# 1/rms of tokens: eleven VectorE steps and a diagonal, or one GpSimd power and a repeated column

## The chip, the cores and the metric

The kernel runs on one core of a Trainium2 chip. The metric is the device time in microseconds of one execution. The core has five engines with a queue each, worked off in order: PE (TensorE; PEld is its weight loading), DVE (VectorE), ACT (ScalarE), POOL (GpSimd) and SP, which here only issues DMAs.

## The reference

One layer of a hybrid decoder on 16 meta tokens and 1024 real tokens of width 1024, in float32. Three mixers run side by side on the normalised input, then a SwiGLU layer and a last normalisation follow:

```python
def rmsnorm(x, g):
    y = x * lax.rsqrt(jnp.mean(x * x, axis=-1, keepdims=True) + EPS)
    return y * g
...
hn = rmsnorm(h, mix_norm_g)
sb_q, sb_k, sb_v, ssm_z, ssm_xbc, ssm_dt, c_q, c_kv, k_r = split(hn @ w_in)
o_sb  = stick_breaking_attention(sb_q, sb_k, sb_v)      # 8 heads of 64
o_ssm = ssd_mixer(ssm_z, ssm_xbc, ssm_dt, ...)          # Mamba-2; ends in rmsnorm(y * silu(z), norm_g)
q  = rmsnorm(c_q,  q_norm_g)  @ w_uq                    # latents of width 384
kv = rmsnorm(c_kv, kv_norm_g) @ w_ukv                   # and of width 256
o_mla = mla_attention(q, kv, rope(k_r))                 # 8 heads
h = h + concat(o_sb, o_ssm, o_mla) @ w_out
fn = rmsnorm(h, ffn_norm_g)
h = h + (silu(fn @ w_gate) * (fn @ w_up)) @ w_down
return rmsnorm(h, final_norm_g)
```

So 1/rms per token is needed for the input, for both latents, for the gated state-space output, for the feed-forward input and for the output.

## The kernel before

Activations lie with features on the partitions and tokens along the free dimension. Each dense product is three TensorE products: operands are split into a rounded part and a rest (`hi`, `lo`), and hi·hi, lo·hi and hi·lo are added up in PSUM. ScalarE makes the rounded part; the rest is a subtraction, in most places on GpSimd.

The sum of squares of a token runs over partitions, so `token_rstd` takes it with TensorE: for each block of 128 tokens the squares are the weights and a column of ones moves, which leaves the sums as one column per block with tokens on the partitions (`ps`, up to 9 columns). `rstd_columns` then makes mean square plus epsilon on VectorE (L172), and `col_rsqrt` makes 1/√x there: a shift and a multiply-add on the bits for a first guess, and three Newton rounds of three instructions, all on a tile of 2 to 9 columns. `spread` turns the columns into a row repeated on all partitions: per block VectorE scales the identity by the column (`dg`, L180), and TensorE multiplies it with a tile of ones (L181).

Eleven places use this:

- `chunk_rstd`, three times, for the three token chunks of the input (pool `p0`, 3 blocks each). The first projections run on the input without 1/rms, and their results are scaled by `row` when they are taken out of PSUM (L585) or by the column `r` (L572); then `normalise` scales the input itself.
- `column_rstd`, three times: for both latents (`latent_units`), while the chunks of the state-space scan (`ssd_chunk`) run, and for the gate of its output (`gate_units`) beside the last attention heads. `spread_row` spreads them.
- `row_sums` and `row_spread`, twice, ahead of the feed-forward products, for each half of the tokens.
- `last_part` and `last_row`, three times, at the end, for 512, 256 and 256 tokens. The last of these takes its sums in PSUM banks of its own and calls `col_rsqrt` itself (tile `rl`).

A planner orders each engine's queue: it goes through the program with its own estimates of durations and takes what is ready and has priority. `tc.high_priority(offset=...)` moves instructions forward, and stands around most of the steps above. `tc.issue_after(ins)` puts the instructions of a block that are on the same engine behind `ins`. Around the feed-forward normalisations the order is steered by such marks:

```python
with tc.high_priority(offset=400):
    r = row_sums(acc)
    summed = last_on(PE)
    row = row_spread(*r)
    rowed, rowed_dve = last_on(PE), last_on(DVE)
```

`rowed_dve` is the last VectorE instruction there: before the change the last `dg`. The four VectorE instructions of L1406 stand behind it.

Of the kernel before, what the change touches and what calls it, by code (L numbers as in the profile page):

```python
# [11 lines left out]
F32 = mybir.dt.float32  # L12
F32R = mybir.dt.float32r
BF16 = mybir.dt.bfloat16
I32 = mybir.dt.int32
AF = mybir.ActivationFunctionType
ALU = mybir.AluOpType
AX = mybir.AxisListType
# [3 lines left out]
D = 1024  # L22
# [14 lines left out]
EPS = 1e-6  # L37
# [22 lines left out]
def tile_hybrid_block(ctx: ExitStack, tc: tile.TileContext, a: dict):  # L60
    nc = tc.nc
    act, dve, pool, pe, sp = nc.scalar, nc.vector, nc.gpsimd, nc.tensor, nc.sync
# [11 lines left out]
    const = ctx.enter_context(tc.tile_pool(name="const", bufs=1))  # L74
# [22 lines left out]
    ident = const.tile([128, 128], F32, name="ident")  # L97
# [3 lines left out]
    ones = const.tile([128, 128], F32, name="ones")  # L101
# [2 lines left out]
    dve.memset(zcol, 0.0)  # L104
    halfcol = const.tile([128, 1], F32, name="halfcol")
    dve.memset(halfcol, 0.5)
    sb_mask = const.tile([128, 128], BF16, name="sb_mask")
    mla_mask = const.tile([128, 128], BF16, name="mla_mask")
    for m, base in ((sb_mask, -1), (mla_mask, 0)):
# [30 lines left out]
            with tc.high_priority(offset=1000):  # L140
                evac(ps, c0, n)

    def col_rsqrt(r, x, tmp):

        ri, xi = r.bitcast(I32), x.bitcast(I32)
        dve.tensor_scalar(ri, xi, 1, None, ALU.arith_shift_right)
        dve.tensor_scalar(ri, ri, -1, 0x5F3759DF, ALU.mult, ALU.add)
        for _ in range(3):
            dve.tensor_tensor(tmp, r, r, op=ALU.mult)
            dve.scalar_tensor_tensor(tmp, x, -0.5, tmp, ALU.mult, ALU.mult)  # L150
            dve.scalar_tensor_tensor(r, tmp, 1.5, r, ALU.add, ALU.mult)

    def token_rstd(cols, ps, squares, blocks, width, bufs=1):


        for e, (t0, w) in enumerate(blocks):
            for i, sq in enumerate(squares):
                pe.matmul(
                    ps[:w, e : e + 1], sq[:, t0 : t0 + w], ones[:, 0:1], start=(i == 0), stop=(i == len(squares) - 1)
                )  # L160
        return rstd_columns(cols, ps, blocks, width, bufs)

    def rstd_columns(cols, ps, blocks, width, bufs=1):
        nb = len(blocks)
        x, r, t = (cols.tile([128, nb], F32, tag=f"rc{i}{nb}", bufs=bufs, name="rc") for i in range(3))
        e0 = 0
        if blocks[0][1] < 128:
            w = blocks[0][1]
            dve.memset(x[:, 0:1], 1.0)
            dve.tensor_scalar(x[:w, 0:1], ps[:w, 0:1], 1.0 / width, EPS, ALU.mult, ALU.add)  # L170
            e0 = 1
        dve.tensor_scalar(x[:, e0:nb], ps[:, e0:nb], 1.0 / width, EPS, ALU.mult, ALU.add)  # L172
        col_rsqrt(r, x, t)
        return r

    def spread(diag, row, r, blocks, t0, wide=None, bufs=2):

        for e, (b0, w) in enumerate(blocks):
            dg = diag.tile([128, 128], F32, tag="dg", bufs=bufs, name="dg") if wide is None else wide[:, 128 * e : 128 * (e + 1)]
            dve.tensor_scalar(dg[:w, :w], ident[:w, :w], r[:w, e : e + 1], None, ALU.mult)  # L180
            pe.matmul(row[:, b0 - t0 : b0 - t0 + w], ones[:w, :], dg[:w, :w], start=True, stop=True)  # L181

    dpool = ctx.enter_context(tc.tile_pool(name="dpsum", bufs=2, space=PSUM))
    tp_st = ExitStack()
# [2 lines left out]
    def bank():  # L187
        return dpool.tile([128, 512], F32, tag="d", name="d_ps")
# [10 lines left out]
    def fill_tile(tag, name):  # L199
        return fl.tile([128, 388 if tag == "craw" else 384], F32, tag=tag, name=name)  # L200
# [7 lines left out]
    p0 = p0_st.enter_context(tc.tile_pool(name="p0", bufs=1))  # L208
# [36 lines left out]
    def chunk_rstd(i):  # L245
        c0, n = CH_ALL[i]
        blocks = [(t0 - c0, w) for t0, w in BLOCKS[3 * i : 3 * i + 3]]
        acc = fill_tile("cacc", "acc")[:, :n]
        for k in range(KT):
            x = xT[:, k, c0 : c0 + n]  # L250
            sq = acc if k == 0 else sqs[k % 2][:, 512 * (k // 2 % 2) :][:, :n]
            act.activation(sq, x, AF.Square)
            if k > 0:
                dve.tensor_tensor(acc, acc, sq, op=ALU.add)
        ssum = ps0.tile([128, 4], F32, tag="ssum", name="ssum")
        with tc.high_priority(offset=200):
            r = token_rstd(p0, ssum, [acc], blocks, D, bufs=3)
            rrow = ps0.tile([128, 512], F32, tag="rrow", bufs=1, name="rrow")
            spread(p0, rrow, r, blocks, 0, bufs=3)
            row = fill_tile("craw", "row")  # L260
            act.copy(row[:, :n], rrow[:, :n])
        return r, row
# [373 lines left out]
    for i, (q0, qn) in enumerate(((0, 256), (256, 384), (640, 384))):  # L636
# [3 lines left out]
        c0, n = CH_ALL[i]  # L640
        r, row = stats[i]
# [59 lines left out]
    def spread_row(row, r, blocks, chunks, scale=1.0):  # L701
        for c0, m in chunks:
            ps = bank()
            inside = [e for e, b in enumerate(blocks) if c0 <= b[0] < c0 + m]
            spread(ga, ps, r[:, inside[0] : inside[-1] + 1], [blocks[e] for e in inside], c0)
            act.activation(row[:, c0 : c0 + m], ps[:, :m], AF.Copy, scale=scale)

    def heads(ap, h=8):
# [2 lines left out]
    ga = ctx.enter_context(tc.tile_pool(name="ga", bufs=1, side="right", reuse_waits="tile"))  # L711
    grow = ga.tile([128, T], F32, name="grow")
    with ExitStack() as st:
# [118 lines left out]
        def row_tile(name):  # L832
            return la.tile([128, T], F32, tag="lraw", bufs=4, name=name)
# [39 lines left out]
        for b, (t0, w) in enumerate(BLOCKS):  # L873
            ps = bank()
# [6 lines left out]
            t = row_tile("vtok")  # L881
# [18 lines left out]
        for c0, n in CH_SHORT:  # L900
# [4 lines left out]
            for half, (op, ta, tb) in enumerate(((ALU.subtract, ct, sn), (ALU.add, sn, ct))):  # L905
                t = fill_tile("cacc", "rope")
# [155 lines left out]
    def ffn_bank():  # L1062
        return pp.tile([128, 512], F32, tag="b", name="b_ps")
# [8 lines left out]
    def add(out, x, y, eng=None):  # L1072
        (eng or dve).tensor_tensor(out, x, y, op=ALU.add)  # L1073
# [10 lines left out]
    def q_tile(name):  # L1084
        return tq.tile([128, 512], F32, tag="q", name=name)

    def row_sums(squares):
        blocks = [(128 * b, 128) for b in range(4)]
        r = token_rstd(ga, bank(), squares, blocks, D)
        return r, blocks  # L1090

    def row_spread(r, blocks):
        ps = bank()
        spread(None, ps, r, blocks, 0, q_tile("dg"))
        return ps

    def normed(k, c):
# [132 lines left out]
# [4 lines that stand above are left out]
# [161 lines left out]
# [5 lines that stand above are left out]
    T3 = []  # L1400
    for i in range(4):

        t = q_tile("T3")
# [67 lines left out]
    def next_raw(src):  # L1471
        nonlocal nraw
        pl = fr if nraw % 16 < 8 else f2
        nraw += 1
        return raw_tile(pl, src)
# [82 lines left out]
    p0 = 0  # L1558
# [10 lines left out]
    for e, f in enumerate(range(2 * p0, NF)):  # L1569
        w, h = next_raw(a["w_down"][f]), next_raw(s_hid[f])  # L1570
# [26 lines left out]
    def last_part(t0, n, by_pe=False, between=None):  # L1597

        ts = slice(t0, t0 + n)
        blocks = [(128 * b, 128) for b in range(n // 128)]  # L1600
        squares, sums = [], []

        def column_sums(o):
            if o == 0:
                sums.extend(ffn_bank() for _ in blocks)
            for (b0, w), ps in zip(blocks, sums):
                pe.matmul(ps[:, 0:1], squares[o][:, b0 : b0 + w], ones[:, 0:1], start=(o == 0), stop=(o == KT - 1))

        for o in range(KT):
            down(o, t0, n)  # L1610
            if o == 2 and between:
                row = last_row(*between)
            sq = q_tile("tt")[:, :n]
            act.activation(sq, hT[o][:, ts], AF.Square)
            if by_pe:
                squares.append(sq)
                if o >= 3:
                    column_sums(o - 3)
            elif o == 0:
                squares.append(sq)  # L1620
            else:
                add(squares[0], squares[0], sq, dve if o >= 5 else pool)
        if by_pe:
            for o in range(KT - 3, KT):
                column_sums(o)
        with tc.high_priority(offset=1000):
            if sums:
                x, r, t = (ga.tile([128, len(blocks)], F32, tag=f"rl{i}", name="rl") for i in range(3))
                for e, ps in enumerate(sums):
                    dve.tensor_scalar(x[:, e : e + 1], ps[:, 0:1], 1.0 / D, EPS, ALU.mult, ALU.add)  # L1630
                col_rsqrt(r, x, t)
            else:
                r = token_rstd(ga, bank(), squares, blocks, D)
        return (r, blocks), row if between else None

    def last_row(r, blocks):
        row = bank()
        with tc.high_priority(offset=100):
            spread(None, row, r, blocks, 0, q_tile("dg"))
        return row  # L1640

    def last_norm(t0, n, row, by_pool, ng):
# [15 lines left out]
    r0, _ = last_part(0, 512)  # L1658
    r1, row = last_part(512, 256, between=r0)
    last_norm(0, 512, row, (3, 6), 2)  # L1660
    r2, row = last_part(768, 256, True, r1)
# [92 lines left out]
```

## Time and profile before

| | |
|---|---|
| median of 3 runs | 1889.12 us (1889.0 to 1889.23) |
| profiled execution | 1887.26 us, span 1885.5 us |
| mean granted TensorE clock | 0.962 |
| busy: PE, PEld | 1730.0 us, 1501.6 us |
| busy: DVE, ACT, POOL | 1322.4 us, 866.0 us, 880.6 us |

The span runs from the first to the last instruction; times in the timeline count from its start. In a timeline line stand the start, the duration, the engine, the source line, the operation, its output and inputs by the names of the program, and the shape; "x4" is a run of four such instructions. A bracket at the end tells how long the engine stood idle before it, and what it waited for. SPq is the DMA issue on SP. Groups by line give the count, busy time, and the mean duration in ns; the view of one source line gives the shortest, median and longest duration in ns. The chain that ended last is followed back from the last instruction, at each step to what released it.

### The profile page before, as it was taken

Reading aid. Unit: us, or ns where it says so; the run is one execution under the profiler, and the core shown is the slowest. Engines: PE = TensorE matmul, PEld = TensorE weight load, DVE = VectorE, ACT = ScalarE, POOL = GpSimd, SP = SyncE. Lnnn points to the kernel's source line nnn. Section 1 sums busy time; section 2 is a strip of 40 time slices with the busy share of each in tenths; the row PEclk is TensorE's granted clock in tenths of the full one; section 3 lists DMA queues with packets and bytes.
Section 4 is the critical chain, followed back from the end, with each engine's and each line's share of the span. In section 5 each row is a group of like instructions: output and inputs, shape, how many; then the busy total and the mean of one; then the engine's idle time right before and its main releaser. Section 6 shows DMA issues by size and latency. Waiting matters only on the chain.

```text
span 1885.5 us, 26687 instructions
## 1 busy us (share of the span) xinstructions
PE 1730.0 (92%) x9724; PEld 1501.6 (80%) x9724; DVE 1322.4 (70%) x2025; ACT 866.0 (46%) x1881; POOL 880.6 (47%) x707
## 2 busy tenths in 40 slices
PE   8889999999999889996989778889999999799997
PEld 7879989999877679985878657678888888677787
DVE  8888567776546734455565699986667766899956
ACT  7555555555566546674444234432222223433333
POOL 3443244243565465553221266653344333688782
PEclk9999999999999989997999889999999999899998
DMA  4221132122634554454332513122222224733102
GB/s 151 56 73 64 57 80 74 52 60 72 167 105 139 180 164 106 107 130 150 57 72 91 129 50 112 49 86 79 82 88 83 76 75 136 280 100 109 47 0 90
DMA packets 124615, 182.75 MB, mean 97 GB/s; under 512 B 29490, under 2 KB 86804, under 8 KB 124484
## 3 DMA queue, kind: packets, MB, share of 16 engines
q1 hardware_dynamic: 105088, 165.49, 29.3%
q10 hardware_dynamic: 19396, 15.56, 2.7%
q8 instruction: 76, 1.25, 0.3%
q14 instruction: 55, 0.45, 0.1%
HBM read 129.51 MB, written 51.50 MB: 96 GB/s over the span
## 4 chain that ended last, share of the span: by engine, by line
PE 61%; DVE 15%; DMA 7%; issue 4%; POOL 3%; ACT 3%; SPq 1%; ACTq 0%; DVEq 0%; POOLq 0%
PE b_ps L1327 7%; PE b_ps L1329 7%; PE b_ps L1328 7%; PE d_ps L137 6%; PE d_ps L139 6%; PE d_ps L138 6%; DVE raw L1070 2%; DMA gy<-s_y 2%; PE b_ps L1528 2%; PE b_ps L1530 2%; PE b_ps L1529 2%; DVE op L1067 2%; PE ptg L325 1%; DMA raw<-s_ossm 1%; PE pv L303 1%
## 5 line engine op out<-in xcount | busy, mean ns | idle before, releaser
L137 PE MATMUL d_ps<-hnh,whi 128*128 128x384 f32 (+6 forms) x744 | 248.9, 335 | 7.8 <-DVE go L535 4.0
L139 PE MATMUL d_ps<-hnl,whi 128*128 128x384 f32 (+6 forms) x744 | 246.1, 331 | 0.0
L138 PE MATMUL d_ps<-hnh,wlo 128*128 128x384 f32 (+6 forms) x744 | 245.9, 331 | 0.0
L126 POOL TENSOR_TENSOR wlo<-wraw,whi 128x1024 fp32r<-128x1024 f32 (+1 forms) x51 | 124.7, 2445 | 180.9 <-ACT whi L124 171.8
L1067 POOL TENSOR_TENSOR op<-raw,op 128x512 fp32r<-128x512 f32 x113 | 174.3, 1573 | 57.2 <-ACT op L1066 54.0
L137 PEld LDWEIGHTS d_ps<-hnh,whi 128*128 128x128 f32 (+1 forms) x744 | 140.9, 189 | 12.9 <-DVE go L535 5.5
L311 DVE TENSOR_TENSOR pl<-ptg,ph 128x512 fp32r<-128x512 f32 (+1 forms) x160 | 99.5, 629 | 64.5 <-ACT ph L310 62.8
L138 PEld LDWEIGHTS d_ps<-hnh,wlo 128*128 128x128 f32 (+1 forms) x744 | 140.7, 189 | 2.3 <-issue 0.2
L139 PEld LDWEIGHTS d_ps<-hnl,whi 128*128 128x128 f32 (+1 forms) x744 | 140.6, 189 | 2.4 <-issue 0.2
L1327 PE MATMUL b_ps<-T,wh 128*128 128x512 f32 x352 | 138.4, 394 | 0.7 <-ACT T L1066 0.7
L1066 ACT CAST op<-raw 128x512 fp32r<-128x512 f32 x149 | 84.1, 618 | 117.2 <-PE d_ps L1530 46.9
L1328 PE MATMUL b_ps<-T,wl 128*128 128x512 f32 x352 | 137.1, 390 | 0.5 <-POOL wl L1067 0.5
L1329 PE MATMUL b_ps<-T,wh 128*128 128x512 f32 x352 | 137.6, 392 | 0.0
L1067 POOL TENSOR_TENSOR wlo<-raw,whi 128x1024 fp32r<-128x1024 f32 (+1 forms) x22 | 53.0, 2410 | 150.5 <-ACT whi L1066 150.5
L670 DVE TENSOR_TENSOR_SCAN cm<-cm,zcol 128x144 f32<-128x144 f32 (+3 forms) x64 | 101.2, 1586 | 13.0 <-ACT cm L668 12.2
L310 ACT CAST ph<-ptg 128x512 fp32r<-128x512 f32 (+1 forms) x160 | 85.6, 543 | 36.7 <-PE ptg L327 28.7
L1067 POOL TENSOR_TENSOR wl<-raw,wh 128x512 fp32r<-128x512 f32 x46 | 70.6, 1545 | 62.2 <-ACT wh L1066 62.2
L1070 DVE TENSOR_TENSOR raw<-raw 128x512 f32<-128x512 f32 x58 | 70.9, 1227 | 40.4 <-DMA raw<-in_w_gate_dram 35.8
L1066 ACT CAST wh<-raw 128x512 fp32r<-128x512 f32 x88 | 53.0, 616 | 73.7 <-PE b_ps L1329 66.0
L492 POOL TENSOR_TENSOR csig<-csig,cacc 128x384 f32<-128x384 f32 (+1 forms) x36 | 47.8, 1328 | 83.0 <-ACT csig L491 50.6
L487 DVE SCALAR_TENSOR_TENSOR cacc<-d_ps,cw,cacc 128x384 f32<-128x384 f32 (+3 forms) x108 | 61.8, 573 | 33.6 <-ACT cacc L480 31.5
L1528 PE MATMUL b_ps<-op 128*128 128x512 f32 x183 | 73.7, 408 | 12.6 <-DVE hF L1073 11.3
(447 smaller groups left out, 5434.3 us busy)
## 6 DMA issues: line engine op xcount, KB each, us to landing
raw<-in_w_gate_dram SPq DMA_DIRECT2D x22, 512.0 KB
raw<-in_w_up_dram SPq DMA_DIRECT2D x22, 512.0 KB
s_hid<-gs SPq DMA_DIRECT2D x44, 256.0 KB
raw<-in_w_down_dram SPq DMA_DIRECT2D x22, 512.0 KB
raw<-s_hid SPq DMA_DIRECT2D x22, 512.0 KB
wraw<-in_w_xbc_dram SPq DMA_DIRECT2D x12, 512.0 KB
wraw<-in_w_o_dram SPq DMA_DIRECT2D x10, 512.0 KB
s_xs<-csig SPq DMA_DIRECT2D x24, 192.0 KB
```

Of the source, the lines that this page charges most:

```text
L126: pool.tensor_tensor(lo[:, :cols], raw[:, :cols], f32(hi[:, :cols]), op=ALU.subtract)
L137: pe.matmul(ps[:m, :n], wh, mh, start=(kt == 0), stop=False)
L138: pe.matmul(ps[:m, :n], wl, mh, start=False, stop=False)
L139: pe.matmul(ps[:m, :n], wh, ml, start=False, stop=(kt == nkt - 1))
L670: dve.tensor_tensor_scan(rev, rev, zcol.to_broadcast([128, n_all]), 1.0, ALU.mult, ALU.add)
L1066: act.copy(hi, value)
L1067: eng.tensor_tensor(lo, value, f32(hi), op=ALU.subtract)
L1070: dve.tensor_tensor(out, x, y, op=ALU.subtract)
L1327: pe.matmul(banks[j], hi[:, ks], UH[u][k], start=start and k == 0, stop=False, skip_group_check=skip)
L1328: pe.matmul(banks[j], lo[:, ks], UH[u][k], start=False, stop=False, skip_group_check=skip)
L1329: pe.matmul(banks[j], hi[:, ks], UL[u][k], start=False, stop=stop and k == 3, skip_group_check=skip)
L1528: pe.matmul(banks[o], wh[:, os], hh, start=first, stop=False, skip_group_check=not start)
```

## The change

`col_rsqrt` and `rstd_columns` go. The mean square is written to one tile `r`, and GpSimd raises it to the power −0.5 in place, with a constant tile of −0.5 as second input. `spread` no longer makes diagonals: the column `r`, repeated 128 times by its access pattern, is the weights, and the identity is the moving side. The tiles `dg` go with them, and with these one use of the pool `tq` in `row_spread` and `last_row`.

```diff
+    mhalf = const.tile([128, 9], F32, name="mhalf")
+    dve.memset(mhalf, -0.5)
...
-    def col_rsqrt(r, x, tmp):
-
-        ri, xi = r.bitcast(I32), x.bitcast(I32)
-        dve.tensor_scalar(ri, xi, 1, None, ALU.arith_shift_right)
-        dve.tensor_scalar(ri, ri, -1, 0x5F3759DF, ALU.mult, ALU.add)
-        for _ in range(3):
-            dve.tensor_tensor(tmp, r, r, op=ALU.mult)
-            dve.scalar_tensor_tensor(tmp, x, -0.5, tmp, ALU.mult, ALU.mult)
-            dve.scalar_tensor_tensor(r, tmp, 1.5, r, ALU.add, ALU.mult)
...
-        dve.tensor_scalar(x[:, e0:nb], ps[:, e0:nb], 1.0 / width, EPS, ALU.mult, ALU.add)
-        col_rsqrt(r, x, t)
+        dve.tensor_scalar(r[:, e0:nb], ps[:, e0:nb], 1.0 / width, EPS, ALU.mult, ALU.add)
+        pool.tensor_tensor(r, r, mhalf[:, :nb], op=ALU.pow)
         return r
 
-    def spread(diag, row, r, blocks, t0, wide=None, bufs=2):
+    def spread(row, r, blocks, t0):
 
         for e, (b0, w) in enumerate(blocks):
-            dg = diag.tile([128, 128], F32, tag="dg", bufs=bufs, name="dg") if wide is None else wide[:, 128 * e : 128 * (e + 1)]
-            dve.tensor_scalar(dg[:w, :w], ident[:w, :w], r[:w, e : e + 1], None, ALU.mult)
-            pe.matmul(row[:, b0 - t0 : b0 - t0 + w], ones[:w, :], dg[:w, :w], start=True, stop=True)
+            pe.matmul(
+                row[:, b0 - t0 : b0 - t0 + w], r[:w, e : e + 1].to_broadcast([w, 128]), ident[:w, :w], start=True, stop=True
+            )
...
-                x, r, t = (ga.tile([128, len(blocks)], F32, tag=f"rl{i}", name="rl") for i in range(3))
+                r = ga.tile([128, len(blocks)], F32, tag="rl", name="rl")
                 for e, ps in enumerate(sums):
-                    dve.tensor_scalar(x[:, e : e + 1], ps[:, 0:1], 1.0 / D, EPS, ALU.mult, ALU.add)
-                col_rsqrt(r, x, t)
+                    dve.tensor_scalar(r[:, e : e + 1], ps[:, 0:1], 1.0 / D, EPS, ALU.mult, ALU.add)
+                pool.tensor_tensor(r, r, mhalf[:, : len(blocks)], op=ALU.pow)
```

The callers lose the arguments for `dg`. With it gone, `rowed_dve` is the mean-square instruction.

More of the change, by code (lines that the diff above doesn't have):

```diff
@@ L14 @@
 BF16 = mybir.dt.bfloat16
-I32 = mybir.dt.int32
 AF = mybir.ActivationFunctionType
@@ L160, in token_rstd @@
                 )
-        return rstd_columns(cols, ps, blocks, width, bufs)
-    def rstd_columns(cols, ps, blocks, width, bufs=1):
         nb = len(blocks)
-        x, r, t = (cols.tile([128, nb], F32, tag=f"rc{i}{nb}", bufs=bufs, name="rc") for i in range(3))
+        r = cols.tile([128, nb], F32, tag=f"rc{nb}", bufs=bufs, name="rc")
         e0 = 0
@@ L168, in rstd_columns @@
             w = blocks[0][1]
-            dve.memset(x[:, 0:1], 1.0)
-            dve.tensor_scalar(x[:w, 0:1], ps[:w, 0:1], 1.0 / width, EPS, ALU.mult, ALU.add)
+            dve.memset(r[:, 0:1], 1.0)
+            dve.tensor_scalar(r[:w, 0:1], ps[:w, 0:1], 1.0 / width, EPS, ALU.mult, ALU.add)
             e0 = 1
-        dve.tensor_scalar(x[:, e0:nb], ps[:, e0:nb], 1.0 / width, EPS, ALU.mult, ALU.add)
-        col_rsqrt(r, x, t)
+        dve.tensor_scalar(r[:, e0:nb], ps[:, e0:nb], 1.0 / width, EPS, ALU.mult, ALU.add)
+        pool.tensor_tensor(r, r, mhalf[:, :nb], op=ALU.pow)
         return r
-    def spread(diag, row, r, blocks, t0, wide=None, bufs=2):
+    def spread(row, r, blocks, t0):
         for e, (b0, w) in enumerate(blocks):
-            dg = diag.tile([128, 128], F32, tag="dg", bufs=bufs, name="dg") if wide is None else wide[:, 128 * e : 128 * (e + 1)]
-            dve.tensor_scalar(dg[:w, :w], ident[:w, :w], r[:w, e : e + 1], None, ALU.mult)
-            pe.matmul(row[:, b0 - t0 : b0 - t0 + w], ones[:w, :], dg[:w, :w], start=True, stop=True)
+            pe.matmul(
+                row[:, b0 - t0 : b0 - t0 + w], r[:w, e : e + 1].to_broadcast([w, 128]), ident[:w, :w], start=True, stop=True
+            )
     dpool = ctx.enter_context(tc.tile_pool(name="dpsum", bufs=2, space=PSUM))
@@ L258, in chunk_rstd @@
             rrow = ps0.tile([128, 512], F32, tag="rrow", bufs=1, name="rrow")
-            spread(p0, rrow, r, blocks, 0, bufs=3)
+            spread(rrow, r, blocks, 0)
             row = fill_tile("craw", "row")
@@ L704, in spread_row @@
             inside = [e for e, b in enumerate(blocks) if c0 <= b[0] < c0 + m]
-            spread(ga, ps, r[:, inside[0] : inside[-1] + 1], [blocks[e] for e in inside], c0)
+            spread(ps, r[:, inside[0] : inside[-1] + 1], [blocks[e] for e in inside], c0)
             act.activation(row[:, c0 : c0 + m], ps[:, :m], AF.Copy, scale=scale)
@@ L1093, in row_spread @@
         ps = bank()
-        spread(None, ps, r, blocks, 0, q_tile("dg"))
+        spread(ps, r, blocks, 0)
         return ps
@@ L1638, in last_row @@
         with tc.high_priority(offset=100):
-            spread(None, row, r, blocks, 0, q_tile("dg"))
+            spread(row, r, blocks, 0)
         return row
```

## The prediction

> **What bounds the kernel now.** I read the page first: its line of busy times, and the first line of the chain that ended last.
>
> ```profile
> PE 1730.0 (92%) x9724; PEld 1501.6 (80%) x9724; DVE 1322.4 (70%) x2025; ACT 866.0 (46%) x1881; POOL 880.6 (47%) x707
> PE 61%; DVE 15%; DMA 7%; issue 4%; POOL 3%; ACT 3%; SPq 1%; ACTq 0%; DVEq 0%; POOLq 0%
> ```
>
> TensorE bounds the whole, but 15% of the chain is VectorE. The change touches only places where 1/rms is made, so I then read the rows of the old steps by source line.
>
> ```profile
> L149 DVE TENSOR_TENSOR rc<-rc x30: 149/161/2261, 20.6 to 1865.8; 128x3 f32<-128x3 f32 x9, 128x4 f32<-128x4 f32 x9, 128x8 f32<-128x8 f32 x6, 128x9 f32<-128x9 f32 x3
> L147 DVE TENSOR_SCALAR rc<-rc x10: 165/172/4694, 18.2 to 1863.7; 128x3 int32<-128x3 int32 x3, 128x4 int32<-128x4 int32 x3, 128x8 int32<-128x8 int32 x2, 128x9 int32<-128x9 int32 x1
> L180 DVE TENSOR_SCALAR dg<-ident,rc x48: 217/280/2269, 25.6 to 1866.6; 128x128 f32<-128x128 f32 x46, 16x16 f32<-16x16 f32 x2
> L181 PE MATMUL d_ps<-dg,ones x82: 258/275/582, 554.1 to 1878.5; 128*128 128x128 f32 x80, 16*128 16x16 f32 x2
>   DVE dg L180: 29.0, 10
> ```
>
> An old step takes about 0.16 us when nothing disturbs it, but up to 4.694 us. The last line is from the view of L181: TensorE's idle time (by its matmul and weight-load queues together) before a spreading product, ended by a diagonal from VectorE, 29.0 us in 10 places. So the small work is on the path in some places, and I went through the timeline of each of the eleven.
>
> **What is removed and added.** Each place loses 11 VectorE instructions (two on integers, nine of Newton) and one diagonal per block, 50 in all (the 48 of the row and two at the end). At median prices that is 11 × 11 × 0.16 + 50 × 0.28 = 33 us of VectorE work, plus the disturbances. Each place gains one GpSimd power on 2 to 9 columns. The spreading products stay: as many products and weight loads. The repeated column is now the weights, the identity the moving side; I take their price as unchanged (0.275 us), because the shapes are the same. VectorE's mean-square instruction stays, and now GpSimd waits for it, with the later operand splits of GpSimd queued behind.
>
> The trace shows no power. Nearest rows, by shape:
>
> ```profile
> L406 POOL TENSOR_TENSOR vst<-vsp,vst 16x128 f32<-16x128 f32 x8 | 3.9, 492 | 14.1 <-DMA vsp<-s_vsb 10.1 <-DMA vst<-s_vsb 3.6 <-PE ptg L327 0.2
> L506 POOL TENSOR_TENSOR grow<-grow,sq 128x256 f32<-128x256 f32 x9 | 6.6, 733 | 7.4 <-ACT sq L505 6.5 <-issue 0.8
> L1651 POOL TENSOR_TENSOR outt<-hF,rstds 128x512 f32<-128x512 f32 x2 | 2.6, 1297 | 3.3 <-ACT rstds L1645 3.3
> ```
>
> From 733 to 1297 ns for 256 more elements is 2.2 ns each, which leaves about 0.17 us fixed. A plain operation on 9 columns would be about 0.2 us: the lower end. If a power is a logarithm, a product and an exponential of some 25 such steps, each at the fixed price, it is 4.3 us: the upper end. I take 1.3 us, nearer to the plain row because these few columns leave only the fixed part of a program inside one instruction. A gain below the lower end is excluded, since the power replaces nothing on GpSimd.
>
> **Place by place, starting with the first projections (3 chunks).**
>
> ```profile
> 49.48 0.15 DVE L172 TENSOR_SCALAR rc<-ssum 128x3 f32<-128x3 f32 x1
> 57.87 0.98 DVE L151 SCALAR_TENSOR_TENSOR rc<-rc 128x3 f32<-128x3 f32 x1
> 68.49 0.16 DVE L151 SCALAR_TENSOR_TENSOR rc<-rc 128x3 f32<-128x3 f32 x1
> 57.02 6.67 POOL L272 TENSOR_TENSOR hnl<-xT,hnh 128x384 fp32r<-128x384 f32 x5 [15.05 <-ACT hnh L270]
> 69.19 1.62 PE L181 MATMUL rrow<-dg,ones 128*128 128x128 f32 x6 [4.64 <-ACT vs L572]
> 71.36 1.02 DVE L585 TENSOR_TENSOR scaled<-d_ps,row 128x384 f32<-128x384 f32 x2 [1.93 <-ACT row L261]
> ```
>
> Chunk 2's mean square is ready at 49.63, but its Newton steps stand between other VectorE work, so r comes at 68.65. TensorE stops for 4.64 us, and VectorE itself for 1.93. GpSimd is idle for 15.05 us before 57.02, so a power there could be done near 51 even at the upper price. The whole 4.64 can go; late next is VectorE, which is full here. The evacuations it must do before chunk 2's would still push some of it back, so I count −3.0 (0 to −4.64). Chunks 0 and 1 count zero: TensorE was busy past them, and that is the cover.
>
> **State-space stage (two places).**
>
> ```profile
> 555.38 2.13 DVE L180 TENSOR_SCALAR dg<-ident,rc 128x128 f32<-128x128 f32 x1 [0.16 <-PE d_ps L181]
> 557.43 1.76 DVE L792 TENSOR_TENSOR L<-L,cbm 128x1024 f32<-128x1024 f32 x1
> 555.01 2.43 POOL L126 TENSOR_TENSOR wlo<-wraw,whi 128x1024 fp32r<-128x1024 f32 x1 [0.39 <-ACT whi L124]
> ```
>
> A diagonal that should take 0.28 us ends with GpSimd's subtraction, 557.51 against 557.44: it waited for it. By the rows alone its removal is worth 2.13. But L792 is next in line and reads two SBUF tensors, so it would meet the same subtraction. The Trainium skill, SBUF — State Buffer, section Who interferes with whom, says that a VectorE instruction with two SBUF inputs or in a two-port mode is blocked for a whole GpSimd instruction, and one with at most one SBUF input is not. By that rule the 2.13 us passes on to L792 and the gain here is 0. I take 0, because the two powers also enter a GpSimd queue that is half full; bounds −5 (this diagonal twice and a little) to +5 (two powers near the upper price on the path, with something behind each).
>
> **Gate (one place).**
>
> ```profile
> 850.54 0.20 ACT L975 ACTIVATION_READ_ACCUMULATOR pr<-sc_ps,sm 128x1 f32 x1
> 846.83 4.69 DVE L147 TENSOR_SCALAR rc<-rc 128x8 int32<-128x8 int32 x1
> 851.56 2.26 DVE L149 TENSOR_TENSOR rc<-rc 128x8 f32<-128x8 f32 x1
> 856.24 0.20 DVE L990 RECIPROCAL inv<-inv 128x8 f32<-128x8 f32 x1
> 856.47 0.37 SPq L991 DMA_DIRECT2D s_inv<-inv  x1
> 862.71 10.12 DMA raw<-s_osb
> 872.85 0.04 ACT raw L1023
> 874.44 0.79 PE L137 MATMUL d_ps<-raw,whi 128*128 128x512 f32 x1 [10.55 <-ACT grow L706]
> 846.80 4.70 POOL L941 TENSOR_TENSOR mlo<-st,mhi 96x1040 fp32r<-96x1040 f32 x2 [1.67 <-ACT mhi L940]
> 851.46 2.34 POOL L1024 TENSOR_TENSOR raw<-raw 128x1024 fp32r<-128x1024 f32 x1
> ```
>
> L147 and L149 run exactly as long as GpSimd's subtractions. Behind them VectorE holds an attention head's reciprocal, whose last input was there at 850.74; the SP queue waits for it with its DMA of 856.47, and with the loads behind that. One of these, issued at 862.71, lands at 872.83 (the two rows of the chain); ScalarE's cast of it (L1023) stands ahead of its copy of grow, which ends TensorE's stop of 10.55 us. Without Newton the reciprocal can run at about 851.2, so −5.2. The power queues behind the subtractions, until 853.80 + 1.3, and TensorE's spread waits for it nearly as long as before; but that holds only products of the old head, with the large stop behind them as cover. I count −4.0 (−5.2 to 0).
>
> **First normalisation of the feed-forward part.**
>
> ```profile
> 1153.66 0.16 DVE L172 TENSOR_SCALAR rc<-d_ps 128x4 f32<-128x4 f32 x1 [0.61 <-PE d_ps L158]
> 1160.83 2.05 PE L181 MATMUL d_ps<-dg,ones 128*128 128x128 f32 x8 [2.77 <-DVE dg L180]
> 1162.91 2.72 DVE L1100 SCALAR_TENSOR_TENSOR hT<-hT,gffn,d_ps 128x512 f32<-128x512 f32 x4 [1.05 <-PE d_ps L181]
> 1145.93 8.97 POOL L1067 TENSOR_TENSOR op<-raw,op 128x512 fp32r<-128x512 f32 x6 [2.50 <-ACT op L1066]
> ```
>
> From mean square to the row's first user: 1162.91 − 1153.82 = 9.1 us, all on the chain. Now: GpSimd free at 1154.90, power 1.3, four spreads 2.05, so the user runs at about 1158.3: −4.6. VectorE was nearly full, so what leaves it counts too and nothing else comes late first. I take −4.0 (−4.6 to −1.6 at the upper price).
>
> **Second normalisation.**
>
> ```profile
> 1178.84 0.15 DVE L172 TENSOR_SCALAR rc<-d_ps 128x4 f32<-128x4 f32 x1
> 1188.13 2.08 PE L181 MATMUL d_ps<-dg,ones 128*128 128x128 f32 x8 [5.78 <-DVE dg L180]
> 1190.22 3.19 POOL L1067 TENSOR_TENSOR wl<-wraw,wh 128x512 fp32r<-128x512 f32 x2 [4.34 <-ACT wh L1066]
> ```
>
> TensorE's 5.78 us would vanish if the power runs at once. But the products behind it need GpSimd's splits of 1190.22 to 1193.41, which the power pushes back by its own length; these are late next. I take −2.0 (−5.8 to +3, the latter at the upper price with nothing won).
>
> **End.**
>
> ```profile
> 1872.78 0.38 DVE L1630 TENSOR_SCALAR rl<-b_ps 128x1 f32<-128x1 f32 x2 [1.03 <-PE b_ps L1607]
> 1877.77 1.20 PE L181 MATMUL d_ps<-dg,ones 128*128 128x128 f32 x4 [4.80 <-DVE dg L180]
> 1870.41 5.51 POOL L1651 TENSOR_TENSOR outt<-hF,rstds 128x256 f32<-128x256 f32 x8 [10.24 <-ACT rstds L1645]
> ```
>
> From the mean squares (1873.16) to the spread 4.6 us pass with nothing beside them. GpSimd works on the output of the chunk before until 1875.92. Put among those eight products, the power saves about 3; put behind them, it ends at 1877.2 and saves about 0.6. I take −1.5 (−3 to +2.4 at the upper price). The two other places at the end count zero: TensorE runs without a stop over them.
>
> **Sum.** −3.0 + 0 − 4.0 − 4.0 − 2.0 − 1.5 = −14.5 us. On the profiled execution's 1887.26 that is 1872.8; the median of the runs is 1.9 above it, so I predict 1874.6. The bounds add up to −28 and +9. About 0.2% (3.8 us) is what a measurement of this kernel can tell from no change.
>
> **Rivals.** *The power is slow.* If GpSimd works a power out element by element, it may be far over my upper end; no row excludes it. The four places that are on the path (chunk 2 has slack) then each pay the excess over 1.3 us, so 14.5 / 4 = 3.6: from about 5 us a power the change loses, at 10 us it gives about 1909. For it: the operation has no neighbour in the trace; against: only few columns. Chance 0.20. *Queues laid out anew.* The planner orders every queue from its own estimates, and 171 instructions gone with 12 new ones move many later ones. VectorE and GpSimd may be interleaved worse in the long stages. Five operand splits of 1.6 us (the last row of the second normalisation) on the path cost 8, and with half of the gains gone the time is about 1890. Chance 0.10. *The gains are passed on.* GpSimd's in-order queue becomes late in place of VectorE's, at the gate and both normalisations; only chunk 2 and the end remain, −4.5, and 1884.6. Chance 0.15. The forecast keeps 0.55.
>
> **How the numbers follow.** The forecast's bounds reach from 1861 to 1898. Above that lies only the slow power, where it costs over 7 us, about half of its chance; so the range is 1860 to 1900, with about 0.1 left out above it and less below. Faster by over 0.2%: the forecast's 0.55, 0.12 of the passing-on and 0.05 of the queues, 0.72. Same: 0.03 of each of these two, 0.06. Slower: the slow power's 0.20 and 0.02 of the queues, 0.22.
>
> **What would show it.** Right: one GpSimd row of 0.5 to 2 us at each place; the stops of 4.64, 2.77, 5.78 and 4.80 us before the spreads gone or below 2; the s_inv DMA about 5 us after the last accumulator no more. Wrong: power rows above 4 us, or spreads that wait for GpSimd as long as they waited for VectorE.

## The result and the profile after

| | before | after |
|---|---|---|
| median of 4 runs each, on one chip | 1889.06 us (1885.44 to 1889.23) | 1874.07 us (1871.96 to 1875.89) |
| ratio of after to before | | 0.9928, 95% interval 0.9913 to 0.9943 |
| profiled execution, span | 1887.26, 1885.5 us | 1874.14, 1872.3 us |
| mean granted TensorE clock | 0.962 | 0.966 |

The changed kernel is 15.0 us faster by the medians, 13.6 by the ratio of the runs; the forecast was 14.5. The kernel before had medians of 1877 to 1889 us on the chips used here, so below each kernel is compared with runs of the kernel before on its own chip, and a ratio is turned into microseconds with that median. Traces of the experiments come from these chips too, and two of them can drift apart without a change of order: p3 and p4 below, with the same queue of TensorE up to 1100 us, by 10 us between 475 and 1075. So what is read from them is stops and orders; a small difference in length alone shows little.

The page of the changed kernel, its busy times and the first line of its chain:

```profile
PE 1738.6 (93%) x9724; PEld 1499.5 (80%) x9724; DVE 1257.8 (67%) x1855; ACT 864.2 (46%) x1881; POOL 889.0 (47%) x718
PE 59%; DVE 17%; DMA 9%; ACT 5%; issue 4%; POOL 4%; SPq 1%; ACTq 0%; DVEq 0%; POOLq 0%
```

VectorE has 65 us and 170 instructions less, GpSimd 8 us more. Yet VectorE's share of the chain did not fall, and DMA's rose from 7 to 9%: a first sign that this is not simply VectorE's small work leaving the path.

The groups of the new lines by shape (count, busy us, mean ns, idle before):

```profile
L161 POOL TENSOR_TENSOR rc<-rc,mhalf 128x4 f32<-128x4 f32 x3 | 3.4, 1141 | 2.5 <-DVE rc L160 2.5
L161 POOL TENSOR_TENSOR rc<-rc,mhalf 128x8 f32<-128x8 f32 x2 | 3.3, 1648 | 1.5 <-DVE sm L960 1.5
L161 POOL TENSOR_TENSOR rc<-rc,mhalf 128x3 f32<-128x3 f32 x3 | 2.9, 964 | 0.0
L161 POOL TENSOR_TENSOR rc<-rc,mhalf 128x9 f32<-128x9 f32 x1 | 1.8, 1797 | 0.0
L161 POOL TENSOR_TENSOR rc<-rc,mhalf 128x2 f32<-128x2 f32 x1 | 0.7, 709 | 7.5 <-DVE rc L160 7.5
L167 PE MATMUL d_ps<-ident,rc 128*128 128x128 f32 x76 | 10.6, 279 | 2.0 <-POOL rc L161 1.6 <-ACT cd L755 0.4
```

The power takes 0.7 to 1.8 us by its number of columns, around the 1.3 that the forecast used, and the spreads hardly stand still: 2.0 us in all for the 76 records of the tile `d_ps` (two for each spread of 128 tokens).

The gate, from the timeline of the changed kernel:

```profile
854.35 0.17 DVE L160 TENSOR_SCALAR rc<-d_ps 128x8 f32<-128x8 f32 x1
854.60 1.65 POOL L161 TENSOR_TENSOR rc<-rc,mhalf 128x8 f32<-128x8 f32 x1 [1.50 <-DVE sm L960]
856.30 2.05 PE L167 MATMUL d_ps<-ident,rc 128*128 128x128 f32 x16 [1.58 <-POOL rc L161]
858.55 1.09 ACT L694 ACTIVATE grow<-d_ps 128x512 f32<-128x512 f32 x2
858.89 0.20 DVE L978 RECIPROCAL inv<-inv 128x8 f32<-128x8 f32 x1
859.47 1.47 SPq L979 DMA_DIRECT2D s_inv<-inv  x1
860.24 1.04 ACT L1011 CAST raw<-raw 128x1024 fp32r<-128x1024 f32 x1
```

All eight spreads run as one batch 2 us after the mean square, ScalarE copies `grow` at once, and only then comes its cast that may have to wait for a DMA. Before, that cast stood ahead of both copies of `grow` (873.80 and 881.15) and TensorE stopped for 10.55 us; that stop is gone.

Both feed-forward normalisations and the end, from the same timeline:

```profile
1147.04 0.16 DVE L160 TENSOR_SCALAR rc<-d_ps 128x4 f32<-128x4 f32 x1 [1.45 <-PE d_ps L149]
1149.07 1.02 POOL L161 TENSOR_TENSOR rc<-rc,mhalf 128x4 f32<-128x4 f32 x1
1153.89 1.05 PE L167 MATMUL d_ps<-ident,rc 128*128 128x128 f32 x8
1154.98 2.73 DVE L1088 SCALAR_TENSOR_TENSOR hT<-hT,gffn,d_ps 128x512 f32<-128x512 f32 x4 [0.20 <-PE d_ps L167]
1171.56 0.15 DVE L160 TENSOR_SCALAR rc<-d_ps 128x4 f32<-128x4 f32 x1
1171.79 1.39 POOL L161 TENSOR_TENSOR rc<-rc,mhalf 128x4 f32<-128x4 f32 x1 [2.50 <-DVE rc L160]
1174.90 1.06 PE L167 MATMUL d_ps<-ident,rc 128*128 128x128 f32 x8
1861.44 0.38 DVE L1618 TENSOR_SCALAR rl<-b_ps 128x1 f32<-128x1 f32 x2 [1.03 <-PE b_ps L1595]
1863.79 0.70 POOL L1619 TENSOR_TENSOR rl<-rl,mhalf 128x2 f32<-128x2 f32 x1
1864.54 1.22 PE L167 MATMUL d_ps<-ident,rl 128*128 128x128 f32 x4 [2.92 <-POOL rl L1619]
```

At the first normalisation the row's first user still comes 7.8 us after the mean square (9.1 before): the power is done at 1150.1, but TensorE works off other products until 1153.9. At the end the power waits 2 us for GpSimd's outputs, and the stop of 4.80 us is 2.92.

Where the time went between the two traces, by the start of TensorE's instructions that stand in both (median of each stretch of 25 us; plus is later than before):

| at (us of before) | 75 | 125 | 450 | 700 | 800 | 875 | 1100 | 1225 | 1600 | 1850 | end |
|---|---|---|---|---|---|---|---|---|---|---|---|
| after minus before | -2.9 | +1.4 | +5.0 | +7.6 | +8.2 | -11.4 | -11.9 | -12.2 | -10.3 | -11.4 | -13.2 |

The first stage's gain is there at 75 and lost by 125, the long stages lose 8 us, the gate and what lies behind it win 19, the feed-forward norms nothing, and the gate and up loop (1225 to 1600) loses 2. Of the 19, about half is at the gate: between the same instructions TensorE idles 10.4 us less from 840 to 960 us, and 9.9 us less from 960 to 1130, where no step of the change is. The sum came out as forecast, and hardly one term of it did.

Where the 8 us are lost, three stops stand out in the changed kernel. From the view of TensorE's waits in 475 to 700 us (total, times, longest), and from the timeline of GpSimd:

```profile
PE yo L785 <- DVE y L795: 7.0, 2, 5.5
PE d_ps L138 <- DVE rot L895: 6.6, 1, 6.6
```

```profile
630.59 1.90 POOL L724 TENSOR_TENSOR y<-xs,dsk 128x1024 f32<-128x1024 f32 x1 [7.28 <-DMA s_y<-y]
```

GpSimd waits 7.28 us until the old `y` is stored, then VectorE for its `y`, then TensorE for 5.5 us. The kernel before has no stop of TensorE at `yo` there, and its longest two are these:

```profile
PE d_ps L137 <- DVE rot L907: 5.4, 1, 5.4
PE yd L801 <- DVE L L792: 4.9, 5, 1.5
```

The wait at `yd` is 0.7 us in the changed kernel. So the stops have moved more than grown: from 475 to 700 us TensorE idles 22.8 us before and 24.0 between the same instructions after. The other 3.6 of the 4.8 us lost in this stretch are busy time, with a granted clock of 0.95 in place of 0.98.

### The profile page after: what moved, and what is told of

Its sections match the earlier page's. It is cut to its first block, busy times and chain, and to the rows that moved or that the text cites. A ratio compares the mean times of both kernels' runs of the same rounds, so it can differ in the third digit from the quotient of the medians.

```text
span 1872.3 us, 26538 instructions
## 1 busy us (share of the span) xinstructions
PE 1738.6 (93%) x9724; PEld 1499.5 (80%) x9724; DVE 1257.8 (67%) x1855; ACT 864.2 (46%) x1881; POOL 889.0 (47%) x718
## 4 chain that ended last, share of the span: by engine, by line
PE 59%; DVE 17%; DMA 9%; ACT 5%; issue 4%; POOL 4%; SPq 1%; ACTq 0%; DVEq 0%; POOLq 0%
PE b_ps L1316 6%; PE b_ps L1315 6%; PE b_ps L1317 6%; PE d_ps L138 6%; PE d_ps L139 6%; PE d_ps L140 6%; DVE raw L1058 2%; DMA gy<-s_y 2%; DVE op L1055 2%; PE b_ps L1516 2%; PE b_ps L1518 2%; PE b_ps L1517 2%; PE ptg L313 1%; PE pv L292 1%; PE pv L291 1%
## 5 line engine op out<-in xcount | busy, mean ns | idle before, releaser
L1061 DVE TENSOR_TENSOR hF<-hF,b_ps 128x512 f32<-128x512 f32 (+1 forms) x96 | 59.2, 635 | 41.2 <-PE b_ps L1582 21.8
L1516 PE MATMUL b_ps<-op 128*128 128x512 f32 x183 | 73.4, 406 | 11.9 <-DVE hF L1061 10.8
```

The source lines that it names most:

```text
L1516: pe.matmul(banks[o], wh[:, os], hh, start=first, stop=False, skip_group_check=not start)
```

## The experiments

All kernels below are the kernel before with two sets of places. A place in `POWER` takes the GpSimd power, else the Newton steps; a place in `COLUMN` takes the repeated column, else diagonals. The places are `chunk` (the three first chunks), `ck` and `cq` (the latents), `gate`, `ffn1`, `ffn2`, and `last0`, `last512`, `last768`. ALL stands for all nine names. With both sets empty it is the kernel before, with ALL in both the changed one.

```diff
+    if site in POWER:
+        pool.tensor_tensor(r, r, mhalf[:, :nb], op=ALU.pow)
+    else:
+        col_rsqrt(r, x, t)
...
+    if site in COLUMN:
+        pe.matmul(row[:, b0 - t0 : b0 - t0 + w], r[:w, e : e + 1].to_broadcast([w, 128]), ident[:w, :w], start=True, stop=True)
+        continue
```

**Which place, which half.** Theory 1: each place is worth what its own stop was worth. Theory 2: the planner's new order decides, and the places don't add up. Within the change: Newton gone (1a) or diagonals gone (1b). The first four kernels ran on one chip, before at 1884.14 us.

```diff
+POWER = {"gate"}
+COLUMN = {"gate"}
```

> The change at the gate alone (power and repeated column), the other ten places with Newton steps and diagonals as before. Theory 1, direct: each place is worth what its own stop was worth; the time shift between the two traces falls by about 19 us at the gate, from +8 to -11, so this kernel alone gives about -15 to -19 us, 1870 to 1874, since the +8 of the long stages ahead of the gate comes from the other places and is not there. Theory 2, queues laid out anew: the 19 us are where the new order of the queues happens to fall, and with the other places as before the head's output products stop again; then -3 to -6 us by the reciprocal alone, 1883 to 1886. My forecast's own term was -4.

Measured: 1876.77 us, ratio 0.9965 (0.9951 to 0.9979), -6.6 us. Far from the 19 us that the table shows at the gate.

```diff
+POWER = ALL - {"gate"}
+COLUMN = ALL - {"gate"}
```

> The change everywhere but at the gate, which keeps Newton steps and diagonals. Theory 1, direct: what the places other than the gate are worth together: +8 by the long stages, about 0 at the two feed-forward norms, -2 at the end, so +2 to +6 us over before, 1891 to 1895, and e1 and this add up to the whole change's -15. Theory 2, queues laid out anew: the two do not add up; this one anywhere between 1875 and 1900. My forecast's terms without the gate's were -10.5, 1878.5.

Measured: 1882.55 us, ratio 0.9996 (0.9983 to 1.0008), -0.8 us. Together with the gate alone -7.4, where the whole change has -13.6 by its ratio: they do not add up, so theory 1 falls as a whole; its forecasts for both kernels were missed too.

```diff
+POWER = ALL
+COLUMN = {}
```

> The power at all eleven places, the diagonals and their products with ones as before. If the gate's gain is the Newton steps gone from in front of the attention head's reciprocal (theory 1a), this has most of the gain, 1874 to 1879. If it is the batch of eight spreads and the early copy of grow, which need the diagonals and their two buffers gone (theory 1b), the stop of ScalarE's copy of grow behind its cast is still there and the gain is -2 to -6, 1883 to 1887.

Measured: 1886.74 us, ratio 1.0015 (1.0001 to 1.0029), +2.8 us.

```diff
+POWER = {}
+COLUMN = ALL
```

> Newton steps on VectorE kept at all eleven places; the repeated column in place of the diagonals everywhere. Theory 1a: next to nothing at the gate, 1885 to 1891. Theory 1b: all eight spreads run as one batch as soon as Newton is done, the copy of grow gets ahead of the cast, and the stop of 10.55 us goes: -8 to -13, 1876 to 1881.

Measured: 1865.02 us, ratio 0.9898 (0.9879 to 0.9918), -19.2 us, more than either theory said. The half of the change without the power is faster than the whole, and the power alone is, if anything, slower than before. The gate in the timeline of this kernel (L198 is the repeated column, L158 Newton, L729 the copy of grow, L1046 the cast):

```profile
843.14 3.36 PE L198 MATMUL d_ps<-ident,rc 128*128 128x128 f32 x14 [4.71 <-DVE rc L158]
859.10 1.04 ACT L1046 CAST raw<-raw 128x1024 fp32r<-128x1024 f32 x1 [10.09 <-DMA raw<-s_osb]
860.20 0.80 PE L144 MATMUL d_ps<-raw,whi 128*128 128x512 f32 x1 [5.40 <-ACT raw L1046]
```

Newton still costs TensorE 4.71 us here and the cast 5.40. In the whole change the spreads wait 1.58 us (shown above) and the product behind that cast 2.69:

```profile
887.19 0.80 PE L138 MATMUL d_ps<-raw,whi 128*128 128x512 f32 x1 [2.69 <-ACT raw L1011]
```

So at the gate the power does help; the loss must be elsewhere.

**Where the power loses.** The next four ran on another chip, before at 1885.0 us.

```diff
+POWER = {}
+COLUMN = {"gate"}
```

> The repeated column at the gate alone, Newton steps kept there, everything else as before; all queues are those of before up to the gate. Theory A (the diagonals are what cost, Newton steps are not): as much as the whole change at the gate alone, -6 to -9 us against before. Theory B (Newton steps in front of the attention head's reciprocal cost, my forecast): 0 to -2 us.

Measured: 1881.27 us, ratio 0.9982 (0.9968 to 0.9997), -3.4 us: between the two theories.

```diff
+POWER = {"ck", "cq"}
+COLUMN = ALL
```

> The repeated column at all places; the power at the two latents of the state-space stage only, Newton steps at the other nine. Theory C (the power is bad in the state-space stage, where its kernels show TensorE waiting 5.5 to 6 us for y ahead of yo and 6.6 to 8 us for rot): -19 us of the column alone less some 8 to 13, so -6 to -11 against before. Theory D (the power costs a little at each of its places, or by the order of the first stage on): -17 to -19.

Measured: 1856.66 us, ratio 0.9850 (0.9832 to 0.9869), -28.3 us. Against both theories: with the power at the latents the kernel does not lose but wins some 9 us over the column alone. The traces of the two, 6 us apart, do not show that gain at the latents: from 475 to 960 us this kernel takes 5 us longer. It wins behind that, where TensorE's queue has the same order in both: 2.8 us up to 1130, 4.2 between 1240 and 1600, and 4.7 from there to 1840.

```diff
+POWER = ALL - {"ck", "cq"}
+COLUMN = ALL
```

> The whole change less the power at the two latents, which keep Newton steps; TensorE's queue is that of the whole change. Theory C: the loss of the power in the state-space stage comes back, -19 to -24 against before. Theory D, and the rival that the order of the queues holds the loss (which is the same here): -13 to -15, as the whole change, or a little less because Newton's steps come back.

Measured: 1869.37 us, ratio 0.9917 (0.9896 to 0.9937), -15.6 us, as the whole change. The state-space stage loses in this kernel and has no power in it, so theory C falls: what it has in common with the whole change is the power ahead of it, in the first chunks, and the order of TensorE's queue.

```diff
+POWER = {"last0", "last512", "last768"}
+COLUMN = ALL
```

> The repeated column at all places; the power at the three last places only, Newton steps elsewhere. The queues are those of the column alone up to the last stage. My forecast gave the end -1.5 us by the power; from the mean square to the spread it was 4.6 us before, 3 in the whole change. So -1 to -3 against the column alone, -20 to -22 against before. If the column alone already has what is to be had there: 0, -19.

Measured: 1865.93 us, ratio 0.9897 (0.9880 to 0.9914), -19.4 us, no more than the column alone. But the trace shows the forecast gain at the end. The last spread in the timeline of the column alone, then of this kernel:

```profile
1853.19 1.19 PE L198 MATMUL d_ps<-ident,rl 128*128 128x128 f32 x4 [4.29 <-DVE rl L158]
```

```profile
1853.32 1.02 PE L198 MATMUL d_ps<-ident,rl 128*128 128x128 f32 x4 [2.92 <-POOL rl L161]
```

The stop is 1.4 us shorter, and between 1700 and 1850 us this kernel wins 3.9 us over the column alone. It had lost some 4.5 before, evenly over the gate and up loop, where the instructions are the same.

That loop gave the next question. In it TensorE is full, without a stop, and its granted clock is 1.00, and still its 512-wide products start every 0.2295 us in three kernels (before, e4, f1), 0.2268 in two (e1, f2) and 0.2318 to 0.2323 in five (the whole change, e2, e3, f3 and f4; from the timelines, 1560 to 1610 products each). The classes go with the places of the tiles in SBUF: the change adds a constant (`mhalf`, which takes 64 bytes per partition and moves the weights' tiles on the left side) and takes tiles away on the right side. This bears on the halves: 0.0023 us more for each of some 1600 products is about 3.7 us, which is more than the +2.8 of the power alone (e3, 0.2318), and two thirds of the 5.6 us by which the whole change lies behind the column alone (e4, 0.2295).

**Order or place.** These three ran on a third chip, before at 1877.07 us.

```diff
+        const.tile([128, 16], F32, name="lpad")
```

> The kernel before with one unused tile of 64 bytes per partition among its constants: every queue is word for word that of before, only the tiles of the left side of SBUF (weights and their halves) lie 64 bytes higher, as they do in the changed kernel by its new constant. Theory P (the rate of TensorE's 512-wide products depends on where their operands lie): in the gate and up loop the products start every 0.2295 us in before, e4 and f1, 0.2268 in e1 and f2, 0.2319 in the whole change and e2, e3, f3, which are three classes by the places of the tiles; this kernel has the places of e1 and f2, so 0.2268 and -4.3 us over the 1590 products there; over the whole run -2 to -6 us, unless earlier stages lose. Rival (chance from execution to execution, or the order of the queues): 0.2295 and 0 +- 2 us.

Measured: 1871.93 us, ratio 0.9967 (0.9954 to 0.9979), -6.2 us, and 0.2268 us a product in the loop. The kernel before becomes 0.3% faster by 64 unused bytes.

```diff
+POWER = ALL
+COLUMN = ALL
...
+        ga.tile([128, 16], F32, tag="pad", name="rpad")
```

> The whole change with one unused tile of 64 bytes per partition on the right side of SBUF, which puts the feed-forward part's operands where e1 and f2 have them; every queue is that of the whole change. Theory P: 0.2319 becomes 0.2268 in the loop, -8 us over its 1590 products, so -21 to -24 against before instead of -13.6 to -15. Rival: as the whole change, -13.6 to -15.

Measured: 1861.74 us, ratio 0.9914 (0.9895 to 0.9933), -16.1 us, and 0.2316 in the loop: a miss. The places of e1 and f2 were met by the remainder by 128 bytes, not by 256: most moving operands lie at 224 (by 256) and their weights at 96, where e1, f2 and p1 have 96 for both. The products of p2 sorted by that: 0.2277 us where both lie at 96, 0.2331 where they lie 128 apart.

```diff
+POWER = ALL - {"chunk"}
+COLUMN = ALL
...
+        ga.tile([128, 16], F32, tag="pad", name="rpad")
```

> The whole change with Newton steps kept in the three chunks of the first projections (the repeated column there too), and the same 64 bytes as p2. Theory L (the power in the first chunks gives every later queue another order, with TensorE's 5.5 us wait for y ahead of yo and the 6.6 us wait for rot in the state-space stage, 8 us lost by the multi-head latent stage): those waits are gone as in the column alone, and it is 6 to 10 us faster than p2, -28 to -34 against before, the fastest of all. Rival (each place's own stops decide): the first chunks' power was worth -3 there, so it is 0 to 3 us slower than p2.

Measured: 1850.20 us, ratio 0.9846 (0.9826 to 0.9867), -28.9 us: 12.8 us faster than p2, by nothing but the Newton steps put back into the three first chunks. The places of the loop's operands and its rate (0.2315) are those of p2. TensorE's waits from 475 to 700 us in p2, then in p3:

```profile
PE yo L825 <- DVE y L835: 7.4, 2, 5.8
PE d_ps L147 <- DVE rot L935: 6.3, 1, 6.3
PE R L793 <- ACT L L805: 4.4, 4, 1.4
```

```profile
PE d_ps L147 <- DVE rot L935: 4.7, 1, 4.7
PE yd L829 <- DVE L L820: 3.5, 5, 1.2
PE R L793 <- ACT L L805: 1.8, 2, 1.4
PE yo L825 <- DVE y L835: 1.1, 1, 1.1
```

The wait for `y` goes from 7.4 to 1.1 us, more than 500 us behind the chunks. It parts all 14 kernels: 6.7 to 9.4 us in the five with the power in the first chunks (the whole change, e2, e3, f3, p2), at most 1.7 in the nine others. The instructions of this stage are the same in p2 and p3; only their order in the queues differs, and behind some 700 us TensorE's queue is the same. So theory L holds for the waits. Not all of the price is shown to be theirs: from 475 to 700 us TensorE idles 22.0 us in p2 and 14.9 between the same instructions of p3, and another 3.3 us of that stretch are products that ran at a granted clock of 0.98 in place of 0.95. The profiled execution of p3 was the fastest of its five.

**The best version**, on a fourth chip, before at 1882.09 us:

```diff
+POWER = {"ck", "cq", "gate", "last0", "last512", "last768"}
+COLUMN = ALL
...
+        ga.tile([128, 24], F32, tag="pad", name="rpad")
```

> The repeated column at all places; the power at the two latents, the gate and the three last places; Newton steps kept in the first chunks and at the two feed-forward norms; an unused tile of 96 bytes on the right side, which puts both operands of the loop's products at the same remainder by 256 bytes (96), as in p1 and f2 (in p2 and p3 they lay 128 apart, and the loop went at 0.2316 and 0.2315). Theory P: 0.2268 in the loop, -7 us against p3 there; Newton steps at the two norms with the column -3 us against p3 (the column alone took 6 us out of that stretch, p2 and p3 about 2); in all -36 to -40 us against before. Rival (the place does not set the rate): 0.2315 and -29 to -32.

Measured: 1847.09 us, ratio 0.9815 (0.9799 to 0.9830), -34.8 us, the fastest of all though less than the 36 to 40 expected, and 0.2268 in the loop as theory P says. The Newton steps at the two norms were no gain but lost 2.7 us against p3 between 1125 and 1225 us, where TensorE idles 3.5 us more (1130 to 1240): a miss. The loop by rows, the view by windows over 1420 to 1570 us, in before, the changed kernel, p1, p2 and p4 (the length, then the busy time and the count of PE, PEld, DVE, ACT and POOL, then the granted clock; the last two numbers are the DMA share and its GB/s):

```profile
1420.00:1570.00 150.00, 150.00 (x655) 122.63 (x654) 102.07 (x115) 43.30 (x70) 54.92 (x32) 1.00 0.25 81
```

```profile
1420.00:1570.00 150.00, 150.00 (x649) 121.19 (x648) 99.94 (x116) 43.01 (x69) 54.69 (x31) 1.00 0.26 83
```

```profile
1420.00:1570.00 150.00, 150.00 (x663) 124.20 (x663) 103.62 (x119) 44.79 (x72) 56.13 (x32) 1.00 0.26 85
```

```profile
1420.00:1570.00 150.00, 150.00 (x650) 121.49 (x649) 104.02 (x119) 44.11 (x71) 56.17 (x32) 1.00 0.27 85
```

```profile
1420.00:1570.00 150.00, 150.00 (x663) 124.09 (x662) 104.73 (x122) 44.77 (x73) 54.25 (x33) 1.00 0.30 100
```

655, 649, 663, 650 and 663 products in the same 150 us, all with TensorE full at clock 1.00.

## Why the prediction was right, and where it was not

The time was 0.5 us off the forecast, the mechanism only half. Step by step:

- **What is removed.** The forecast put the eleven VectorE steps and the 50 diagonals into one account of 33 us. The halves taken apart are -19.2 us for the column without the power and +2.8 for the power without the column. This is the step that failed: what paid was taking the diagonals out, and the power won nothing in sum. That holds though some 3.7 us of the +2.8 are places in the loop. How much of the 19.2 is the diagonals' own waiting and how much the order that the queues took then was not told apart.
- **The price of the power**, 1.3 us: right (0.70 to 1.80). The rival of a slow power falls. Of the signs of being right, one failed: the stop at the end is 2.92 us, not below 2.
- **First projections, -3.0.** The stop of 4.64 us is gone and the stage runs 3 us ahead, as forecast. That the gain would stay was wrong: it is lost by 125 us, and the power there costs 12.8 us in all (p3 against p2). Up to about 700 us the queues come out in another order, and 7.1 us of TensorE's waiting between 475 and 700 go with it. That is the mechanism of the rival with the queues laid out anew, with a price above its 8; it did not decide the sign, because the other places were worth more than forecast.
- **State-space stage, 0 (-5 to +5).** In the whole change right: without the power at the latents (f3) it is -15.6 against -13.6, intervals overlapping. Added to the column alone the same two powers come with 9 us less, but in the traces the stage itself grows, and the gain lies behind 960 us, 4 of it in the loop with its places; it is not shown to be theirs. The rule of the Trainium skill that was weighed there (SBUF — State Buffer, Who interferes with whom) was tested by no run of its own. The trace of the changed kernel agrees with it where it can be read: the instruction that the prediction names (L792, now L780) took 1.21 to 1.23 us in the eleven cases in which no GpSimd instruction was running at its start; in the five others it ended 1.1 us after the GpSimd instruction did, and took 1.5 to 2.4.
- **Gate, -4.0 (-5.2 to 0).** The stage runs 8 us late when it gets there, and the reciprocal only 2.65 (858.89 against 856.24), so it comes 5.3 us earlier: as forecast. The term was mis-sized because the spreads were said to wait nearly as long as before, and because I did not see that eight spreads in one batch bring the copies of `grow` ahead of ScalarE's cast: 19 us in the table, half of them at the gate itself. The kernels with the power at the gate and the latents have that step too (p2, p3, p4: 16 to 20 us). The gate alone is worth 6.6 us, no more than the 64 bytes that it brings along (p1: 6.2): it wins 11 us at the gate and loses most of them at a stop of 11.65 us at 972 us, before a product of the same line. Why was not settled.
- **Feed-forward norms, -4.0 and -2.0.** Together about 0. At the first, the step "user at about 1158.3" failed: the power waits 1.9 us for GpSimd, and TensorE's queue has 3.8 us of other products ahead of the spread. At the second the stop of 5.78 is gone and one of 2.40 before its sums has come. Against Newton steps with the column (p4) the power is worth 2.7 there.
- **End, -1.5 (-3 to +2.4).** 1.9 us of the stop is gone, 1.8 in the table. Right, and between the two orders that the forecast named: the power waits 2 us for GpSimd's outputs.

So that the sum of -14.5 was met is luck: its errors cancelled. It lacked a cost of 12.8 us by the first chunks and one of some 3.5 us in the loop by the places of the tiles, and its gains at the gate and by the diagonals were too small. With the Newton steps kept in the first chunks (and 64 unused bytes, as in p2) the change is worth 28.9 us (p3).

## What to carry to other kernels

Where a planner writes the queues, an edit in an early stage is also an edit of later ones, here up to some 600 us behind it: price it by leaving out its earliest place, not by the stop that it removes. Take a change with two halves apart before believing a story for the whole; here the repeated column, which the forecast treated as a detail, brought 19 us by itself and the power none, because what it cost in the first chunks was about as much as it brought elsewhere (p2 and p3 against the column alone). And when two kernels differ by less than 1%, move the tiles of one by an unused 64 bytes first: that alone was worth 0.3%.

## What was not expected of the hardware

- The rate of TensorE's 512-wide products, with no stop and at clock 1.00, was 0.2268, 0.2295 or 0.2319 us by where the operands lie in SBUF. Both at the remainder 96 by 256 bytes gave 0.2268 in e1, f2, p1 and p4; 128 apart gave 0.2331 (p2). It is not simply equal remainders: in the kernel before, products with both at 32 took 0.2296 and those with 96 and 32 took 0.2294. What sets it stays open.
- A power on GpSimd took about 0.4 us and 0.155 us for each column of 128 partitions (0.709 for two columns, 1.797 for nine), so that eleven Newton steps of 0.16 us would cost as much as nine columns.
